# A decoder layer on one core: block sums moved from GpSimd to VectorE, the second half of x turned when it is due, gates stored before their sigmoid

## The chip, the core and the metric

The kernel runs on one core of a Trainium2 chip. A core has TensorE (PE: matrix products into PSUM, eight banks of 128 partitions x 512 float32), VectorE (DVE), ScalarE (ACT: functions and copies), GpSimd (POOL), and SyncE (SP), which here only issues transfers. Each engine works through its own queue in order; engines wait for each other by semaphores. The metric is the device time of one execution in microseconds (us), the median over the runs.

## The reference

One layer on a sequence of 1024 rows x 1024 columns, all in float32. x is normalised by row, scaled and shifted by vectors made from `c` (the modulation), and multiplied by a wide weight matrix `w_in`, whose columns are cut into ten parts. An attention branch (8 heads of 64, a mixture of three dilated windows) and a gated recurrence branch (8 heads of 128, in chunks) follow. Each is gated, multiplied by its own matrix, and the two are added under sigmoid gates `g_a` and `g_b`:

```python
h = rmsnorm(x, norm_g) * (1.0 + scale[:, None]) + shift[:, None]
proj = h @ w_in
q_a, k_a, v_a, z_a, q_b, f_b, i_b, z_b, g_a, g_b = jnp.split(proj, cuts, axis=-1)
o_a = dilated_attention(q_a, k_a, v_a, rel_bias) * silu(z_a)
o_b = rmsnorm(hgrn2_recurrence(silu(q_b), f_b, i_b, lb), hgrn_onorm_g) * silu(z_b)
y = sigmoid(g_a) * (o_a @ w_branch_a) + sigmoid(g_b) * (o_b @ w_branch_b)
return rmsnorm(x + gate[:, None] * (y @ w_out), final_g)
```

## The kernel before, in words

**Products in three parts.** A float32 product is made of three products of rounded parts: every operand is split into a high part (`hi`, an ACT copy to a rounded type) and a low part (`lo = a - hi`, a subtraction on DVE, helper `sub`, L224). `mm3` (L238 to L241) issues the three matrix instructions. Nearly all PE work is such 128x512 matrix instructions.

**Seven products for eight.** The projection h @ w_in is worked off in pairs of 128-column blocks (`add_pair`, L265): the 2x2 block product of weights and h takes seven products of 12 matrix instructions instead of eight. For that h, cut into blocks b11, b12 (first 512 columns of the model axis, first and second 512 rows), b21 and b22, is needed split, and with it four sums of blocks, t1 to t4, split as well. Weight sums (`w_s`) are made on DVE as each product is prepared.

**The stream.** The steps of all pairs stand in one queue, `stream`. `stream.step()` issues a quarter of a product (three matrix instructions) and prepares weights two products ahead. The attention and the recurrence, which have waits of their own, call `fill(amount)` between their parts, so that the PE gets a certain number of such steps there. `fill.rate` spreads the steps evenly; `fill.limit` (`in_attention`, `in_gating`) is how far the queue may go. The order of instructions on PE is as the code issues them. On the other engines a scheduler chooses the order, except between `region = ExitStack()` (L511) and `region.close()` (L773), where the written order holds there too.

**The stages**, with their times in the profile of before. (1) The start, 0 to 90 us: the eight row tiles of x are loaded, their row norms taken (`norm_x`), scaled (`scale_x`), transposed on PE (`turn_x`, two PSUM banks for a tile) and copied to `xt` (`keep_x`); the modulation comes from `w_ada` in four parts, each a `modulate(c)`: two halves of 16 small matrix records (`mod_row`), an ACT copy to a row, and a transposition by four tiny products (`mod_turn`). `make_h(j, th)` then makes one of 16 pieces of h and its split: ACT writes `hi`, DVE the value and `lo`. `first_products(j)` are 18 matrix instructions, for three blocks of 128 columns, as soon as piece j is there; all eight are 144. `bias_row` and `bias_add` make the table of the attention's bias. `warm(n)` issues idle products. (2) From 90 us the unit `"first"` (48 matrix instructions for the block VA+P), then the first pair, qk1. (3) Attention with filler, to about 474 us. (4) The branch product of a, with filler ahead of it, to about 560 us. (5) The recurrence with filler, to about 979 us. (6) The branch product of b, the merge and the output, to the end.

**What the change touches.** The sums t1 to t4 are made on GpSimd, in pieces of 128x512 (`sum_1`, `blocks`, `block_4`, L639 to L649), and split by `store_sum` (L634) on ACT and DVE. Two weight splits at the start have their `lo` on GpSimd too (`split_first(1, nc.gpsimd)`, L699, L701). The gates g_a and g_b go through a sigmoid as they leave PSUM (`ev_sigmoid`, L399) and are stored to DRAM (`ga_d`, `gb_d`); they are read back in `branch_a` (L960) and `branch_b` (L1182). The sigmoid and the attention's exponential (L859) need different tables on ACT, and a row ACT_TABLE_LOAD stands at each change between them.

Of the kernel before, what the change touches and what calls it, by code (L numbers as in the profile page):

```python
# [19 lines left out]
P = 128  # L20
# [159 lines left out]
def hybrid_layer(ctx: ExitStack, tc: tile.TileContext, x, w_ada, b_ada, w_in, w_branch_a, w_branch_b, w_out,  # L180
# [218 lines left out]
    def ev_sigmoid(dst, times=False):  # L399

        def ev(src, th, psum):
            t = ctile() if psum or times else src
            nc.scalar.activation(t, src, AF.Sigmoid)
            if times:
                out_ = t if psum else src
                nc.vector.tensor_tensor(out_, src, t, ALU.mult)
                t = out_
            nc.sync.dma_start(dst[:, half_of(th)], t)
        return ev
# [81 lines left out]
    add_unit(w_in_k, VA + P, lambda kh, th, k: [t[:, k] for t in X[NAMES[kh, th]]], ev_v(1), "first")  # L491
    stx = ExitStack()
    sp = stx.enter_context(tc.tile_pool(name="start", bufs=1, side="right"))
    with ExitStack() as st:
# [23 lines left out]
        xs = []  # L518
# [6 lines left out]
        def load_x(t):  # L525
            xs.append(lp.tile([P, D], F32, name=f"x{t}"))
            nc.sync.dma_start(xs[t], x[t * P:(t + 1) * P, :])
# [9 lines left out]

        def mod_row(c, a):
            ps = px.tile([P, 512], F32, name=("pmod", "pxt")[a])
            for k in range(KT):  # L540
                g = 32 * (k % 4)
                nc.tensor.matmul(ps[g:g + 32, 0:256], scz[:, k], was[c][2 * a + k // 4][:, k % 4],
                                 start=k < 4, stop=k >= 4)
            nc.scalar.copy(rows[a], ps[:, 0:256])

        def mod_turn(c, a):
            js = slice(2 * c, 2 * c + 2)
            ps = px.tile([P, 512], F32, name=("pmod", "pxt")[a])
            for n in range(2):
                nc.tensor.matmul(ps[:, n:n + 1], rows[a][:, n * P:(n + 1) * P], ones[:, 0:1], start=True, stop=True)  # L550
            if a == 0:
                nc.vector.tensor_tensor(mods[:, 0, js], ps[:, 0:2], b1[:, js], ALU.add)
                nc.vector.tensor_tensor(mods[:, 0, js], mods[:, 0, js], sm[:, C_G + 2 * c:C_G + 2 * c + 2], ALU.mult)
            else:
                nc.vector.tensor_tensor(mods[:, 1, js], ps[:, 0:2], sm[:, C_B + 2 * c:C_B + 2 * c + 2], ALU.add)

        def modulate(c):
            for a in range(2):
                mod_row(c, a)
            for a in range(2):  # L560
                mod_turn(c, a)

        def norm_x(t):
            if t % 2 == 0:
                nc.scalar.activation(junk[0], xs[t], AF.Square, accum_out=ss[:, t:t + 1])
            else:
                nc.vector.tensor_tensor_reduce(junk[1], xs[t], xs[t], 1.0, 0.0, ALU.mult, ALU.add, ss[:, t:t + 1])
            nc.vector.tensor_scalar(rs[:, t:t + 1], ss[:, t:t + 1], 1.0 / D, EPS, ALU.mult, ALU.add)
            nc.gpsimd.tensor_tensor(rs[:, t:t + 1], rs[:, t:t + 1], half[:, 0:1], ALU.pow)

        def scale_x(t):
            if t % 2:
# [4 lines left out]
        def split_first(n, engine=nc.vector):  # L577
            hi, lo = (wpool.tile([P, 4, P], F32R, name=name) for name in ("w_hi", "w_lo"))
            nc.scalar.copy(hi, stream.tiles[ids[n]])
            engine.tensor_tensor(lo, stream.tiles[ids[n]], hi.bitcast(F32), ALU.subtract)  # L580
# [34 lines left out]
        def make_h(j, th):  # L615
            hj = xt[th][:, j]
            hi, lo = X[NAMES[j // 4, th]]
            nc.scalar.activation(hi[:, j % 4], hj, AF.Identity, bias=mods[:, 1, j:j + 1], scale=mods[:, 0, j:j + 1])
            nc.vector.tensor_scalar(hj, hj, mods[:, 0, j:j + 1], mods[:, 1, j:j + 1], ALU.mult, ALU.add)
            sub(lo[:, j % 4], hj, hi[:, j % 4])  # L620
# [13 lines left out]
        def store_sum(name, k, got):  # L634
            hi, lo = X[name]
            nc.scalar.copy(hi[:, k], got)
            sub(lo[:, k], got, hi[:, k])

        def sum_1(k):  # L639
            t = ctile()  # L640
            nc.gpsimd.tensor_tensor(t, xt[1][:, k], xt[0][:, k], ALU.subtract)
            return t

        def blocks(k):
            nc.gpsimd.tensor_tensor(xt[1][:, k], xt[1][:, k + 4], xt[1][:, k], ALU.subtract)
            nc.gpsimd.tensor_tensor(xt[0][:, k], xt[1][:, k], xt[0][:, k], ALU.add)

        def block_4(k):
            nc.gpsimd.tensor_tensor(xt[0][:, k + 4], xt[0][:, k + 4], xt[0][:, k], ALU.subtract)  # L649
# [757 lines left out]
```

## Time and profile before

| | |
|---|---|
| median of 3 runs | 1168.54 us (1166.1 to 1171.85) |
| the profiled execution | 1164.41 us, span 1162.6 us |
| mean granted TensorE clock | 0.987 |
| PE busy | 1114.2 us, 96% of the span |
| DVE busy | 826.7 us, 71% |
| ACT busy | 549.7 us, 47% |
| POOL busy | 143.9 us, 12% |

The span runs from the first to the last instruction of one execution; its own time is 1.8 us longer, and 4.1 us under the median of the runs. How to read the lines that follow: a line of the waits reads "engine, its line of the code <- engine that released it: us in total, times, longest". A line of the timeline starts with the start and the duration in us; at its end, in brackets, stands how long the engine had been idle and what ended that. A matrix instruction's duration (0.39) overlaps with the next one's; the pitch from start to start is what it costs. A line of the windows gives, for a stretch of time, the busy time of each engine, the granted clock (PEclk, 1.00 is full) and the share of the transfer engines. A line of the groups gives the number of instructions, their busy time in all and the mean in ns. Line numbers (L239) are those of the code above.

### The profile page before, as it was taken

The page shows a single profiled execution, that of the slowest core. Times are in us where ns is not written, and L with a number is a line of the kernel's source. Part 1 is how long each engine was busy: PE and PEld are TensorE (multiplying, and loading weights), DVE is VectorE, ACT ScalarE, POOL GpSimd, SP SyncE. Part 2 cuts the span into 40 slices and gives each one's busy share as a digit, 9 for nine tenths or more (in the row PEclk, how much of TensorE's full clock was granted, in tenths as well). Part 3 has the DMA queues.
Part 4 walks back from the last instruction along what each step waited for, and adds up shares of the span by engine and source line. Part 5 has one row for each costly group of instructions (what it writes and reads, how often), then busy time and mean ns, then how long its engine had stood idle before and what let it go on. Part 6 is the DMA issues. An engine that isn't in the chain of part 4 may idle for free.

```text
span 1162.6 us, 21691 instructions
## 1 busy us (share of the span) xinstructions
PE 1114.2 (96%) x8278; PEld 912.2 (78%) x8278; DVE 826.7 (71%) x1622; ACT 549.7 (47%) x1080; POOL 143.9 (12%) x213
## 2 busy tenths in 40 slices
PE   4888999999999999989999999999999999999997
PEld 4666788887788877878877878788887878888886
DVE  4578877878767777753878787878878773679053
ACT  5335655587887876621343434343444433224021
POOL 2055212122122110200000000000000012000000
PEclk9888999999999999999999999999999999999999
DMA  9717776575455442775625354443525279874052
GB/s 319 210 38 215 189 205 169 149 171 143 114 154 159 109 132 76 234 237 185 205 87 182 101 165 147 135 163 103 185 83 180 98 228 324 290 227 144 15 179 75
DMA packets 161480, 189.54 MB, mean 163 GB/s; under 512 B 11312, under 2 KB 107696, under 8 KB 161376
## 3 DMA queue, kind: packets, MB, share of 16 engines
q1 hardware_dynamic: 140080, 153.95, 41.6%
q0 software_dynamic: 20896, 33.60, 11.4%
q8 instruction: 65, 1.06, 0.4%
q10 hardware_dynamic: 400, 0.61, 0.2%
q14 instruction: 39, 0.32, 0.1%
HBM read 129.36 MB, written 58.76 MB: 162 GB/s over the span
## 4 chain that ended last, share of the span: by engine, by line
PE 82%; DVE 4%; ACT 3%; issue 2%; DMA 1%; POOL 0%; POOLq 0%; ACTq 0%; DVEq 0%
PE m L239 17%; PE m L241 16%; PE m L240 16%; PE pq L240 5%; PE pq L239 5%; PE pq L241 5%; PE po L886 3%; PE pp L1042 2%; PE pt L871 2%; PE pss L854 1%; PE pss L853 1%; PE pou L1125 1%; PE pou L1127 1%; PE pou L1110 1%; DMA vq_d<-ct 1%
## 5 line engine op out<-in xcount | busy, mean ns | idle before, releaser
L246 ACT CAST w_hi<-w_raw 128x512 fp32r<-128x512 f32 x146 | 90.5, 622 | 99.3 <-PE m L241 52.6
L224 DVE TENSOR_TENSOR w_lo<-w_raw,w_hi 128x512 fp32r<-128x512 f32 x150 | 105.0, 702 | 40.4 <-ACT w_hi L246 39.7
L246 ACT CAST w_hi<-w_s 128x512 fp32r<-128x512 f32 x90 | 56.1, 623 | 84.4 <-PE m L241 66.7
L327 ACT COPY ct<-m 128x512 f32<-128x512 f32 x90 | 52.7, 585 | 83.3 <-PE m L241 70.6
L274 DVE TENSOR_TENSOR ct<-m,ct 128x512 f32<-128x512 f32 x90 | 61.9, 688 | 23.8 <-PE m L241 22.4
L224 DVE TENSOR_TENSOR w_lo<-w_s,w_hi 128x512 fp32r<-128x512 f32 x90 | 61.9, 687 | 5.7 <-ACT w_hi L246 5.3
L1133 POOL TENSOR_TENSOR ssh<-ssh,halfh 128x4 f32<-128x4 f32 x16 | 16.9, 1057 | 360.6 <-DVE ssh L1132 360.6
L224 DVE TENSOR_TENSOR ptl<-pt,pth 128x512 fp32r<-128x512 f32 (+1 forms) x80 | 50.6, 632 | 13.8 <-ACT pth L875 13.1
L859 ACT ACTIVATE s<-s,st 128x128 f32<-128x128 f32 (+3 forms) x64 | 49.7, 777 | 19.4 <-DVE st L856 19.1
L875 ACT CAST pth<-pt 128x512 fp32r<-128x512 f32 (+1 forms) x80 | 43.5, 543 | 28.3 <-PE pt L871 24.7
L239 PE MATMUL m<-t4h,w_hi 128*128 128x512 f32 x120 | 50.1, 417 | 3.0 <-DVE ct L274 3.0
L239 PE MATMUL m<-b11h,w_hi 128*128 128x512 f32 x124 | 51.7, 417 | 0.0
L239 PE MATMUL m<-t1h,w_hi 128*128 128x512 f32 x120 | 51.0, 425 | 0.0
L239 PE MATMUL m<-b21h,w_hi 128*128 128x512 f32 x124 | 50.9, 411 | 0.0
L239 PE MATMUL m<-b22h,w_hi 128*128 128x512 f32 x124 | 50.9, 410 | 0.0
L239 PE MATMUL m<-t3h,w_hi 128*128 128x512 f32 x120 | 50.2, 418 | 0.0
L856 DVE CUSTOM_DVE_ANT_0 s<-pss,toep 128x512 f32<-128x512 f32 (+2 forms) x64 | 37.3, 587 | 18.0 <-PE pss L854 17.9
L239 PE MATMUL m<-t2h,w_hi 128*128 128x512 f32 x120 | 49.6, 414 | 0.0
L836 POOL DMA_DIRECT2D k<-qk_d x64 | 34.9, 561 | 116.0 <-PE pss L854 112.8
L871 PE MATMUL pt<-kc,s 128*128 128x128 f32 x288 | 44.9, 272 | 4.1 <-DVE s L861 2.1
L241 PE MATMUL m<-b11l,w_hi 128*128 128x512 f32 x124 | 48.8, 393 | 0.0
L241 PE MATMUL m<-b22l,w_hi 128*128 128x512 f32 x124 | 48.7, 393 | 0.0
(352 smaller groups left out, 3299.9 us busy)
## 6 DMA issues: line engine op xcount, KB each, us to landing
w_raw<-in_w_in_dram SPq DMA_DIRECT2D x128, 256.0 KB, 3.3
wa<-in_w_ada_dram SPq DMA_DIRECT2D x16, 512.0 KB, 8.4
qk_d<-ct SPq DMA_DIRECT2D x32, 256.0 KB, 3.3
k<-qk_d POOLq DMA_DIRECT2D x64, 128.0 KB, 4.8
x<-in_x_dram SPq DMA_DIRECT2D x8, 512.0 KB, 7.3
qp<-qk_d POOLq DMA_DIRECT2D x32, 128.0 KB, 4.2
toep<-toep_d POOLq DMA_DIRECT2D x8, 512.0 KB, 6.4
vq_d<-ct SPq DMA_DIRECT2D x16, 256.0 KB, 5.2
```

What stands on the lines that cost most here:

```text
L224: nc.vector.tensor_tensor(out_, a, hi.bitcast(F32), ALU.subtract)
L239: nc.tensor.matmul(ps, ah, bh, start=start, stop=False, skip_group_check=more)
L240: nc.tensor.matmul(ps, al, bh, start=False, stop=False, skip_group_check=more)
L241: nc.tensor.matmul(ps, ah, bl, start=False, stop=stop, skip_group_check=more)
L246: nc.scalar.copy(hi, src)
L274: nc.vector.tensor_tensor(out_, a, b_, op)
L327: nc.scalar.copy(c[name], b[which])
L836: nc.gpsimd.dma_start(dst[c][E * hh:E * hh + E], qk_d[n + hh if dst is qp else n][r, half_of(c)].bitcast(F32R))
L856: nc.vector.tensor_tensor_reduce(s[:, ks:ks + w], ps[:, :w], toep[:, x0:x0 + w][:, ::-1], -1.0, prev, ALU.add, ALU.min, st2[:, a:a + 1])
L859: nc.scalar.activation(s[:, :kw], s[:, :kw], AF.Exp, bias=prev, scale=-1.0, accum_out=st2[:, 2:3])
L871: nc.tensor.transpose(pt[:, c0:c0 + P], pn[b][:, kt * P:(kt + 1) * P], ident)
L875: nc.scalar.copy(pth[:, :w], pt[:, :w])
```

## The change

Five things are changed.

1. t1 to t4 are made on DVE, in place in `xt`, in eight pieces of 128x1024 (`block_sum`). Each has three steps: difference on DVE, `hi` on ACT, `lo` on DVE. A call of `tick()` starts one more piece and does one step of each piece under way; the calls stand between the first products, the evictions and the first steps of the stream. The two weight splits move from GpSimd to DVE.
2. The second half of x (tiles 4 to 7) is loaded into the room of t4, scaled there, and turned late: `turn_late(j)` transposes the four 128x128 pieces that belong to piece j into one PSUM bank, and `make_h` reads that bank. `keep_x` is left out for this half. For j of 2 and over `make_h` makes the value and `hi` on ACT (two instructions) and only `lo` on DVE.
3. `modulate` keeps both halves in one PSUM bank, `pmod`, and turns them in it. The bias rows come before the first products; of the two `warm` calls one is left, at another place.
4. 29 steps of the stream are issued before the attention (16 before), inside the stretch where the order is as written; the pairs are declared earlier. Pair iz0 comes before fq0; the first pair of g_b moves from the recurrence into the attention's part, and fq0 from the attention's part to the one behind it. `fill(6)` becomes `fill(8)` ahead of the branch product of a.
5. g_a and g_b are stored without their sigmoid; it is taken on ACT when they are read. (`ev_silu` is what is left of `ev_sigmoid`.)

```diff
-    def ev_sigmoid(dst, times=False):
...
+    def ev_silu(dst):
         def ev(src, th, psum):
...
+    for m in (0, 2, 4, 6):
+        pair(GA + m * P, GA + m * P + P, ev_raw(ga_d[m]), ev_raw(ga_d[m + 1]))
+    pair(GB, GB + P, ev_raw(gb_d[0]), ev_raw(gb_d[1]))
+    pair_iz(0)
+    in_attention = len(stream.steps)
+    pair_fq(0)
+    pair_fq(1)
+    pair_iz(1)
+    in_gating = len(stream.steps)
...
         def mod_row(c, a):
-            ps = px.tile([P, 512], F32, name=("pmod", "pxt")[a])
+            if a == 0:
+                pmods[c] = px.tile([P, 512], F32, name="pmod")
+            ps = pmods[c][:, 256 * a:256 * a + 256]
...
+        def turn_late(j):
+
+            ps = px.tile([P, 512], F32, name="pxt")
+            for t in range(4):
+                nc.tensor.transpose(ps[:, t * P:t * P + P], xs[4 + t][:, j * P:(j + 1) * P], ident)
+            make_h(j, 1, ps)
...
+            s, b = mods[:, 0, j:j + 1], mods[:, 1, j:j + 1]
+            if j < 2:
+                nc.scalar.activation(hi[:, j % 4], got, AF.Identity, bias=b, scale=s)
+                nc.vector.tensor_scalar(hj, got, s, b, ALU.mult, ALU.add)
+            else:
+                nc.scalar.activation(hj, got, AF.Identity, bias=b, scale=s)
+                nc.scalar.copy(hi[:, j % 4], hj)
             sub(lo[:, j % 4], hj, hi[:, j % 4])
...
+            return [lambda: nc.vector.tensor_tensor(to, a, b_, ALU.subtract),
+                    lambda: nc.scalar.copy(hi[:, s], to), lambda: sub(lo[:, s], to, hi[:, s])]
+
+        sums = [(name, c) for name in ("t1", "t3", "t2", "t4") for c in range(2)]
+        under_way = []
+
+        def tick():
+
+            if sums:
+                under_way.append(block_sum(*sums.pop(0)))
+            for parts in under_way:
+                parts.pop(0)()
+            while under_way and not under_way[0]:
+                under_way.pop(0)
...
-    stream.need("first")
+    for steps in (10, 10, 9):
+        for _ in range(steps):
+            stream.step()
+        tick()
+    region.close()
...
-                fill(6)
+                fill(8)
...
                     nc.sync.dma_start(g[th], ga_d[m][:, half_of(th)])
+                    nc.scalar.activation(g[th], g[th], AF.Sigmoid)
...
                     nc.sync.dma_start(gb[th], gb_d[m][:, half_of(th)])
+                    nc.scalar.activation(gb[th], gb[th], AF.Sigmoid)
```

The order of the instructions, before and after, at three places. The first is PE at the second part of the modulation, `modulate(1)`; a bracket names the semaphores that an instruction waits for (DMAHW: a transfer; Activation: ACT). Before:

```order
L542 MATMUL pmod<-wa_166,scz 32x256 [waits DMAHW4_49]
L542 MATMUL pmod<-wa_166,scz 32x256 x3
L542 MATMUL pmod<-wa_168,scz 32x256 [waits DMAHW5_49]
L542 MATMUL pmod<-wa_168,scz 32x256 x3
L542 MATMUL pxt<-wa_170,scz 32x256 [waits DMAHW6_49,PE_49]
L542 MATMUL pxt<-wa_170,scz 32x256 x3
L542 MATMUL pxt<-wa_172,scz 32x256 [waits DMAHW7_49]
L542 MATMUL pxt<-wa_172,scz 32x256 x3
L550 MATMUL pmod<-ones,row_187 128x1 [waits Activation_49]
L550 MATMUL pmod<-ones,row_187 128x1
L550 MATMUL pxt<-ones,row_188 128x1 [waits Activation_49]
L550 MATMUL pxt<-ones,row_188 128x1
```

The same place of the changed kernel, where both halves stand in `pmod`:

```order
L572 MATMUL pmod<-wa_164,scz 32x256 [waits DMAHW4_49]
L572 MATMUL pmod<-wa_164,scz 32x256 x3
L572 MATMUL pmod<-wa_166,scz 32x256 [waits DMAHW5_49]
L572 MATMUL pmod<-wa_166,scz 32x256 x3
L572 MATMUL pmod<-wa_168,scz 32x256 [waits DMAHW6_49,Activation_49]
L572 MATMUL pmod<-wa_168,scz 32x256 x3
L572 MATMUL pmod<-wa_170,scz 32x256 [waits DMAHW7_49]
L572 MATMUL pmod<-wa_170,scz 32x256 x3
L582 MATMUL pmod<-ones,row_185 128x1 [waits Activation_49]
L582 MATMUL pmod<-ones,row_185 128x1
L582 MATMUL pmod<-ones,row_186 128x1 x2
```

The second half's products now wait for ACT (the copy of the first half's row), and the turning products wait for the copy of the second row.

The second place is DVE from the last piece of h to the weights of the first pair (t1l to t4l: low parts of the sums; `pm`: PSUM of the first products; L430: the eviction of q). Before:

```order
L224 TENSOR_TENSOR b22l<-xt_114,b22h 128x512
L224 TENSOR_TENSOR t1l<-ct,t1h 128x512 x4
L224 TENSOR_TENSOR w_lo<-w_raw_629,w_hi 128x512
L430 SCALAR_TENSOR_TENSOR ct<-pm_0_324,ct 128x512
L430 SCALAR_TENSOR_TENSOR ct<-pm_1_409,ct 128x512
L224 TENSOR_TENSOR w_lo<-w_raw_927,w_hi 128x512
L224 TENSOR_TENSOR ct<-pm_0_325,ct 128x512
L224 TENSOR_TENSOR w_lo<-w_s,w_hi 128x512
L224 TENSOR_TENSOR ct<-pm_1_410,ct 128x512
L274 TENSOR_TENSOR w_s<-w_s,w_raw_927 128x512
L224 TENSOR_TENSOR t2l<-xt_113,t2h 128x512 x4
L224 TENSOR_TENSOR t3l<-xt_114,t3h 128x512 x4
```

The same place of the changed kernel (L679: the difference of a sum; L427: the eviction of q):

```order
L224 TENSOR_TENSOR b22l<-xt_114,b22h 128x512
L224 TENSOR_TENSOR t1l<-xt_113,t1h 128x1024
L679 TENSOR_TENSOR xt_114<-xt_114 128x1024
L224 TENSOR_TENSOR t1l<-xt_113,t1h 128x1024
L679 TENSOR_TENSOR xt_114<-xt_114 128x1024
L224 TENSOR_TENSOR w_lo<-w_raw_545,w_hi 128x512
L224 TENSOR_TENSOR t3l<-xt_114,t3h 128x1024
L679 TENSOR_TENSOR xt_113<-xt_114,xt_113 128x1024
L427 SCALAR_TENSOR_TENSOR ct<-pm_0_313,ct 128x512
L427 SCALAR_TENSOR_TENSOR ct<-pm_1_409,ct 128x512
L224 TENSOR_TENSOR t3l<-xt_114,t3h 128x1024
L679 TENSOR_TENSOR xt_113<-xt_114,xt_113 128x1024
```

The differences now stand among the low parts on DVE, and t3 has moved ahead of the evictions of q.

The third place is PE around the attention's first score (L853 and L854 before, L894 and L895 after; `t1h`, `t3h`: sums of blocks in the products of the pair qk1). Before:

```order
L239 MATMUL m_1002<-t1h,w_hi 128x512
L240 MATMUL m_1002<-t1h,w_lo 128x512
L241 MATMUL m_1002<-t1l,w_hi 128x512
L853 MATMUL pss<-k_911,qp_909 128x128
L854 MATMUL pss<-k_913,qp_909 128x128
L239 MATMUL m_1002<-t1h,w_hi 128x512
```

After:

```order
L241 MATMUL m_1011<-b21l,w_hi 128x512
L894 MATMUL pss<-k_978,qp_976 128x128
L895 MATMUL pss<-k_980,qp_976 128x128
L239 MATMUL m_856<-t3h,w_hi 128x512
L240 MATMUL m_856<-t3h,w_lo 128x512
L241 MATMUL m_856<-t3l,w_hi 128x512
```

The first score, which stood inside the pair's second product, now stands behind its fifth.

More of the change, by code (lines that the diff above doesn't have):

```diff
@@ L536, in load_wa, with mod_turn @@
                     was[c].append(w)
+        pmods = {}
         def mod_row(c, a):
-            ps = px.tile([P, 512], F32, name=("pmod", "pxt")[a])
+            if a == 0:
+                pmods[c] = px.tile([P, 512], F32, name="pmod")
+            ps = pmods[c][:, 256 * a:256 * a + 256]
             for k in range(KT):
                 g = 32 * (k % 4)
-                nc.tensor.matmul(ps[g:g + 32, 0:256], scz[:, k], was[c][2 * a + k // 4][:, k % 4],
+                nc.tensor.matmul(ps[g:g + 32], scz[:, k], was[c][2 * a + k // 4][:, k % 4],
                                  start=k < 4, stop=k >= 4)
-            nc.scalar.copy(rows[a], ps[:, 0:256])
-        def mod_turn(c, a):
+            nc.scalar.copy(rows[a], ps)
+        def mod_turn(c):
             js = slice(2 * c, 2 * c + 2)
[L548 to L555, printed above, removed]
+            ps = pmods[c].rearrange("p (a b) -> p a b", a=2)
+            for a in range(2):
+                for n in range(2):
+                    nc.tensor.matmul(ps[:, a, n:n + 1], rows[a][:, n * P:(n + 1) * P], ones[:, 0:1], start=True, stop=True)
+            nc.vector.tensor_tensor(mods[:, 0, js], ps[:, 0, 0:2], b1[:, js], ALU.add)
+            nc.vector.tensor_tensor(mods[:, 1, js], ps[:, 1, 0:2], sm[:, C_B + 2 * c:C_B + 2 * c + 2], ALU.add)
+            nc.vector.tensor_tensor(mods[:, 0, js], mods[:, 0, js], sm[:, C_G + 2 * c:C_G + 2 * c + 2], ALU.mult)
         def modulate(c):
@@ L559, in modulate, with square_x @@
                 mod_row(c, a)
[L560 to L564, printed above, removed]
+            mod_turn(c)
+        def square_x(t, on_act):
+            if on_act:
                 nc.scalar.activation(junk[0], xs[t], AF.Square, accum_out=ss[:, t:t + 1])
@@ L686, in main_banks @@
                 main[u, th] = pm.tile([P, 512], F32, name=f"pm{u}_{th}")
-        for f, t in all_of_x(0):
-            pass
+        norm_x(0)
+        scale_x(0)
+        turn_x(0)
+        norm_x(1)
+        keep_x(0)
+        scale_x(1)
+        turn_x(1)
+        norm_x(2)
+        keep_x(1)
+        norm_x(3)
+        scale_x(2)
+        turn_x(2)
+        split_first(0)
+        for b in range(2):
+            bias_row(b)
+        scale_x(3)
+        turn_x(3)
+        keep_x(2)
+        for b in range(2):
+            bias_add(b)
@@ new lines, in hybrid_layer @@
+        bias_row(2)
+        keep_x(3)
+        bias_add(2)
+        split_first(1)
+        modulate(0)
+        load_wa(2)
+        split_first(2)
+        make_h(0, 0)
+        make_h(1, 0)
+        main_banks(0)
+        for u in range(3):
+            first_products(0, (0,), (u,))
+        first_products(1, (0,))
+        square_x(4, True)
+        root_x(4)
+        square_x(5, True)
+        square_x(7, False)
+        root_x(5)
+        root_x(7)
+        scale_x(4)
+        square_x(6, True)
@@ L690, in hybrid_layer @@
+        scale_x(5)
+        root_x(6)
+        scale_x(7)
+        scale_x(6)
         warm(8)
[L691 to L693 removed]
+        turn_late(0)
         for a in range(2):
[L695 to L708 removed]
@@ L919, in hybrid_layer @@
         fill.limit = in_gating
-        fill.rate = in_attention * 4 / NH / sum((j + 1) * w for j, w in enumerate(ATT_W))
+        fill.rate = (in_attention - stream.at) * 4 / NH / sum((j + 1) * w for j, w in enumerate(ATT_W))
         fill(2.0)
@@ L1003, in load_f @@
         def load_f(h):
+            stream.need(f"f{h}")
             stream.need(f"h{h}")
```

207 lines of the change are left out of this document (82 added, 125 removed).

## The prediction

> **What bounds the kernel now.** I read the page's first table, then what PE waited for, then the windows, then the timeline where the waits lie.
>
> ```profile
> span 1162.6 us, 21691 instructions
> PE 1114.2 (96%) x8278; PEld 912.2 (78%) x8278; DVE 826.7 (71%) x1622; ACT 549.7 (47%) x1080; POOL 143.9 (12%) x213
> ```
>
> PE is the bound: it is busy for all but 1162.6 - 1114.2 = 48.4 us. The change leaves its matrix products as they are, so it can win only idle time of PE and time in which PE ran at less than its full clock. PE's waits say where the idle time lies, the windows where the clock was low:
>
> ```profile
> PE pm L594 <- DVE x L575: 14.2, 4, 7.5
> PE pt L450 <- DVE ct L224: 4.4, 2, 4.2
> PE po L886 <- DVE oa L892: 3.2, 6, 0.8
> PE m L239 <- DVE ct L274: 3.0, 1, 3.0
> ...
> PE pt L871 <- DVE s L861: 2.1, 2, 1.1
> PE pt L871 <- ACT ct L470: 2.0, 1, 2.0
> ...
> PE pt L1139 <- DVE kt L1134: 1.3, 1, 1.3
> ```
>
> ```profile
> core 0: us, PE busy (x) PEld busy (x) DVE busy (x) ACT busy (x) POOL busy (x), PEclk, DMA share, GB/s
> 30.00:40.00 10.00, 8.04 (x36) 6.67 (x37) 5.56 (x11) 3.60 (x6) 2.39 (x4) 0.72 1.12 327
> 70.00:80.00 10.00, 7.36 (x25) 5.46 (x24) 8.76 (x10) 5.14 (x9) 6.28 (x4) 0.67 0.11 31
> 100.00:110.00 10.00, 5.81 (x31) 4.70 (x29) 9.62 (x18) 7.90 (x18) 4.18 (x8) 0.87 1.20 272
> 110.00:120.00 10.00, 8.71 (x36) 6.81 (x35) 5.40 (x17) 4.31 (x13) 2.85 (x4) 0.79 1.02 273
> 500.00:510.00 10.00, 7.31 (x27) 5.89 (x28) 5.21 (x9) 2.70 (x5) 0.00 (x0) 0.83 0.78 246
> 700.00:800.00 100.00, 100.00 (x1181) 81.81 (x1180) 81.58 (x158) 42.69 (x98) 4.03 (x4) 1.00 0.44 143
> ```
>
> The loss stands in the first 120 us and once near 500 us; from 700 to 800 us PE was never idle. I take the change stage by stage.
>
> **1. The start, from the first product to the unit "first".** These lines of the timeline give the two ends, the waits between them and the prices:
>
> ```profile
> 18.89 1.95 PE L613 MATMUL pmod<-ones 128*128 128x128 f32 x16
> 25.17 0.48 PE L628 MATMUL pm<-b11h,w_hi 128*128 128x512 f32 x1
> ...
> 31.14 1.97 PE L594 MATMUL pm<-kc,x 128*128 128x128 f32 x8 [3.12 <-DVE x L575]
> ...
> 39.48 1.06 PE L594 MATMUL pm<-kc,x 128*128 128x128 f32 x8 [0.82 <-DVE x L575]
> ...
> 45.45 1.07 PE L542 MATMUL pmod<-wa,scz 128*32 128x256 f32 x16
> ...
> 46.33 1.05 PE L542 MATMUL pxt<-wa,scz 128*32 128x256 f32 x16
> ...
> 47.31 0.61 PE L550 MATMUL pmod<-ones,row 128*128 128x1 f32 x4
> ...
> 48.34 0.48 PE L628 MATMUL pm<-b12h,w_hi 128*128 128x512 f32 x1
> ...
> 50.61 0.81 PE L655 MATMUL pmod<-oh,rb 32*8 32x384 f32 x2
> 51.99 0.50 PE L628 MATMUL pm<-b11h,w_hi 128*128 128x512 f32 x1
> ...
> 69.54 0.61 PE L631 MATMUL pm<-b21l,w_hi 128*128 128x512 f32 x1 [1.15 <-DVE b21l L224]
> ...
> 75.09 0.63 PE L631 MATMUL pm<-b21l,w_hi 128*128 128x512 f32 x1
> 75.52 0.63 PE L628 MATMUL pm<-b22h,w_hi 128*128 128x512 f32 x1
> ...
> 90.34 0.39 PE L239 MATMUL m<-b11h,w_hi 128*128 128x512 f32 x1
> ...
> 101.33 1.03 PE L450 MATMUL pt<-kc,ct 128*128 128x128 f32 x8
> ```
>
> Prices: at full clock a 128x512 instruction costs (101.33 - 90.34) / 48 = 0.229, at the half clock 75.52 - 75.09 = 0.43; four transpositions cost 1.06 / 2 = 0.53; a bias row (51.99 - 50.61) / 2 = 0.69; a `modulate` 48.34 - 45.45 = 2.89.
>
> In the changed order each `modulate` is a chain. The first half takes 46.33 - 45.45 = 0.88; then the second half waits until the first row is copied, which by the rows lasts 47.31 - 46.33 = 0.98; the second half takes 0.88 and waits 0.98 again; the turning takes 48.34 - 47.31 = 1.03. That is 4.75, or 1.86 more each. Nothing covers it: the products behind it stand in PE's own queue.
>
> First product: 25.17 + 3 x 0.69 for the bias rows that now come ahead + 1.86 for `modulate(0)` - 1.95 for the `warm(8)` that is gone from there = 27.15. (The `warm(6)` only filled a wait.) From there PE has 144 instructions x 0.229 = 33.0; eight `turn_late` x 0.53 = 4.2; three `modulate` x 4.75 = 14.2; a warm(8) at full clock, half of 1.95, 1.0; and waits. One wait I see: tile 6 is scaled last, behind four squares, its root on POOL and two scalings; between 0 (hidden under the 4 us of the first 18 products) and the 3.12 that tile 4 cost before I take 1.8, since the first three tiles are ahead of it. Sum: 27.15 + 54.2 = 81.3.
>
> What else could hold PE here? ACT makes two instructions of a piece instead of one; the prices are here, with those of DVE for the sums:
>
> ```profile
> L403 ACT ACTIVATE ct<-ct 128x512 f32<-128x512 f32 x46 | 29.1, 633 | 12.5 <-DVE ct L274 11.6
> L403 ACT ACT_TABLE_LOAD x20 | 25.7, 1283 | 0.4
> L859 ACT ACT_TABLE_LOAD x20 | 25.7, 1283 | 0.4
> ```
>
> ```profile
> 101.22 2.49 DVE L224 TENSOR_TENSOR t3l<-xt,t3h 128x512 fp32r<-128x512 f32 x4
> ```
>
> ```profile
> 71.45 1.59 POOL L646 TENSOR_TENSOR xt<-xt,xt 128x512 f32<-128x512 f32 x1
> 71.84 1.75 DVE L224 TENSOR_TENSOR b22l<-xt,b22h 128x512 fp32r<-128x512 f32 x1
> ```
>
> Four ACT instructions of about 0.63 for the two halves of a piece are 2.5 us, under the 18 x 0.229 = 4.1 of its products: hidden, each `turn_late` finding its bank read. On DVE a low part costs 2.49 / 4 = 0.62 alone and 1.75 beside GpSimd's sum. The sums and their low parts are 16 instructions of 2 x 0.62 = 1.25, 20.0 us; with about 26 others of 0.62 (low parts of h and of weights, evictions) DVE has 36 us of work between the last four pieces and the pair's third product, in some 44 us. It fits, without the low parts that took 1.75.
>
> Last, the clock. Before, it was low twice in this stretch: (1 - 0.72) x 10 = 2.8 and (1 - 0.67) x 10 = 3.3 us lost. The second time it fell behind a wait of only 1.15 us, among the small products of a `modulate`. The new chains of 4.75 us hold more idle time than that, so I expect one such fall, 3.05, to the bounds of none and of all 144 instructions at 0.43 (29). The unit then starts at 84.3 instead of 90.34: **-6.0** (from -9.1 to +20).
>
> The Trainium skill ("TensorE: Matmul & The Clock Gate", Part 1) has PE fall to half its clock only after an idle window of some 3.4 us; the trace differs, with 1.15 us at 69.54. By that rule no wait above would cost clock, and the sum would be 3.05 lower.
>
> **2. From the unit to the end of the pair's third product.** Before, from 90.34 to the start of the fourth:
>
> ```profile
> 109.30 1.09 PE L450 MATMUL pt<-kc,ct 128*128 128x128 f32 x4 [4.19 <-DVE ct L224]
> ...
> 120.70 0.39 PE L239 MATMUL m<-b22h,w_hi 128*128 128x512 f32 x1
> ...
> 502.69 0.47 PE L239 MATMUL m<-t4h,w_hi 128*128 128x512 f32 x1 [2.98 <-DVE ct L274]
> ```
>
> This is 30.4 us. In it lie the wait of 4.19 for DVE, whose queue held t2 to t4, 1.1 for the first softmax, and by the clocks 0.87 and 0.79 (windows 100 and 110) 1.3 + 2.1; without them 21.7. In the changed order the sums stand ahead of these rows and GpSimd does not slow them; PE works through five whole products before the first score, so the score's loads have about 10 us more. DVE still has some ten instructions of 0.62 ahead of the first score, and PE reaches the softmax's transposition about as soon: I leave the 1.1 as it is and add 1 for low parts that come late. -8.7 + 2.1 = **-6.6**. If DVE or the loads of the head are no earlier than today, PE waits as before: 0.
>
> **3. The attention.** ACT loads tables 20 + 20 times here; in the changed order I count 13 loads in the whole program. About 28 x 1.28 = 36 us of ACT's time go, and 24 sigmoids of 0.63 with them. ACT is no bound, so only the waits count in which PE stood behind it: po behind oa 3.2 (an ACT copy stands ahead of oa) and pt behind s 2.1. I take **-2.0** of these 5.3; the 2.0 behind L470 stays, since iz0 is still last here; on the other side stand 20 filler steps less, at worst one more wait of 2.0.
>
> **4. The branch of a.** At 502.69 PE had run out of filler: of two pairs behind `in_attention` 52 steps can be issued, the attention takes about 18 of them in advance, and 8 x `fill(6)` asks for 48 more. Now three pairs give 80, some 12 are taken, and 8 x `fill(8)` asks for 64 of 68. The wait of 2.98 and the clock of 0.83 behind it, 1.7, go: **-4.7**. Bounds: 0, if DVE waits for the transfers of z and oa as before; the sigmoids of g_a (16 x 0.63) wait for a load each in ACT's queue, with weights' high parts behind them, and could cost up to the 2.98 again.
>
> **5. The rest: 0.** A pair fewer in the recurrence: PE's work for it moves, it is not saved; PE is busy there throughout, at worst one more wait like L1139's 1.3. g_b's sigmoids: 16 x 0.63 of ACT, which is at 43% from 700 to 800 us and lower behind 1000; each is prepared two steps ahead.
>
> **Sum**: -6.0 - 6.6 - 4.7 - 2.0 = -19.3. The profiled execution, 1164.4, would become 1145.1; the median of the runs lies 4.1 above it, so I predict 1168.5 - 19.3 = **1149.2**.
>
> **The rivals.**
>
> (a) The early gain is given back at the first scores: PE arrives earlier, and waits for DVE or for the loads of head 0, and the branch of a keeps its wait. For: DVE was at 9.62 of 10 there, and its order behind the written stretch is the scheduler's. Against: 36 us of work in 44. Left are -6.0 - 2.0: 1160.5.
>
> (b) The clock does not fall at all in stage 1: 1146.2, and with the whole 5.3 of the attention's waits 1143.
>
> (c) Slower: the clock stays at half from the first product to the end of the unit, 192 instructions, because the chains of `modulate` and the single bank of `turn_late` keep breaking PE's work. Each costs 0.20 more, in all 38.4 instead of 3.05: 1168.5 - 19.3 + 35.3 = 1184.5. It decides from (19.3 + 3.05) / 0.20 = 112 of the 192. For: the fall at 69.54 behind 1.15 us. Against: the row at 75.52 lasts 0.63 and that at 90.34 only 0.39, so the clock came back between them, within 15 us, with the chains of the last pieces still going on. The Trainium skill ("TensorE: Matmul & The Clock Gate", "A second HAM failure mode") tells of such a case, PE idling briefly between groups in PSUM banks so that its clock swings; no run here shows it.
>
> (d) No change that can be told: (a), with two more falls of the clock: -8.0 + 6.1 = -1.9, 1166.6.
>
> **How the numbers follow.** A forecast as summed, 0.50; (a) 0.18; (b) 0.17; (c) 0.05; (d) 0.10. A difference under 0.5% (5.8 us) can hardly be told from none with runs that spread over 5.7. Forecast, (a) and (b) are faster, but (a) by only 8.0, so I give a little of it to no change: faster 0.84, same 0.10, slower 0.06. The range reaches from (b) with all of the attention's waits, 1143, less 1.5 for stage 2 without its new wait, to (a) with a wait of 1.3 more: 1141 to 1162.
>
> **What would show it.** Each right: the unit's first L239 near 84 us; no GpSimd sums and no low part of 1.75; b22's first product of qk1 about 12 us earlier than 120.70; 13 table loads; no wait of 3 us on t4 at 500 us. Wrong: a granted clock under 0.8 in most windows from 30 to 90 us, a new wait of several us at the first pss or pt, or PE waiting for a weight's high part in the branch of a.

## The result and the profile after

| | before | changed |
|---|---|---|
| median of 6 runs | 1168.78 us | 1150.82 us (1147.99 to 1151.76) |
| ratio to before, 95% interval | | 0.9841 (0.9823 to 0.986) |
| profiled execution, span | 1164.41, 1162.6 | 1151.74, 1149.9 |
| PE busy | 1114.2 us, 96% | 1113.1 us, 97% |
| table loads on ACT | 43 | 13 |

The change is faster by 1.6%, some 18 us; 1149.2 was forecast. The two profiled executions differ by 12.7 us only: that of before is 4.4 under its median, that of the changed kernel 0.9 above. The terms can be compared only inside these two, so their sum is held against 12.7, and the other 5.3 us are not located.

Some of PE's waits in the changed kernel (each `modulate` waits twice for a row copy, at L582 and, with the same figures, at L572):

```profile
PE pmod L582 <- ACT row L574: 2.0, 4, 0.5
...
PE pt L1182 <- DVE kt L1177: 2.0, 2, 1.3
PE pt L465 <- DVE zs L1184: 1.4, 2, 0.9
```

The waits on oa (3.2) and on v's split (4.4) are nearly or wholly gone; the row copies (L574) are new. The windows by stage, of before and then of the changed kernel (unit "first" to 140 us, attention, branch of a, the rest):

```profile
90.34:140.00 49.66, 44.18 (x207) 36.19 (x206) 42.42 (x87) 29.13 (x62) 15.32 (x21) 0.93 0.83 221
140.00:475.00 335.00, 327.50 (x1742) 273.54 (x1741) 256.12 (x587) 240.85 (x428) 60.33 (x104) 0.99 0.52 142
475.00:545.00 70.00, 67.02 (x288) 54.26 (x287) 40.18 (x63) 21.00 (x36) 7.92 (x15) 0.98 0.76 245
560.00:1162.60 602.60, 593.04 (x5580) 485.51 (x5578) 425.94 (x784) 216.21 (x484) 30.03 (x41) 1.00 0.48 157
```

```profile
85.90:140.00 54.10, 50.10 (x228) 40.19 (x227) 44.55 (x85) 29.88 (x60) 10.20 (x18) 0.97 0.77 225
140.00:475.00 335.00, 334.47 (x1793) 282.11 (x1791) 262.61 (x602) 199.76 (x394) 67.38 (x118) 1.00 0.57 153
475.00:545.00 70.00, 67.55 (x288) 54.40 (x289) 36.74 (x57) 28.81 (x52) 0.11 (x1) 0.98 0.63 203
560.00:1149.90 589.90, 577.87 (x5508) 471.90 (x5506) 415.92 (x772) 211.67 (x479) 31.19 (x41) 1.00 0.49 158
```

Length less the first busy time is PE's idle time: 5.5 and 4.0, 7.5 and 0.5, 3.0 and 2.5, 9.6 and 12.0 (from 545 to 560 us PE is never idle in either kernel). The clock column adds about 1.7 of loss for a half-clock window in before's attention and in each of the two branch stages. So the attention, of which 2.0 was expected, gave 7.0 + 1.7 = 8.7, and the branch of a, of which 4.7 was expected, gave 0.5.

The timeline of PE at the start, changed:

```profile
16.04 1.97 PE L627 MATMUL pm<-kc,x 128*128 128x128 f32 x8 [2.79 <-DVE x L610]
17.94 1.44 PE L698 MATMUL pxt<-oh,rb 32*8 32x384 f32 x2
...
23.86 1.94 PE L572 MATMUL pmod<-wa,scz 128*32 128x256 f32 x16
26.29 1.94 PE L572 MATMUL pmod<-wa,scz 128*32 128x256 f32 x16 [0.49 <-ACT row L574]
28.72 1.87 PE L582 MATMUL pmod<-ones,row 128*128 128x1 f32 x8 [0.49 <-ACT row L574]
32.01 0.79 PE L666 MATMUL pm<-b11h,w_hi 128*128 128x512 f32 x1 [1.42 <-ACT b11h L653]
...
36.04 0.39 PE L669 MATMUL pm<-b11l,w_hi 128*128 128x512 f32 x1
...
40.94 1.07 PE L572 MATMUL pmod<-wa,scz 128*32 128x256 f32 x16
...
44.98 0.42 PE L638 MATMUL pxt<-kc,t4h 128*128 128x128 f32 x2
...
45.37 0.47 PE L666 MATMUL pm<-b12h,w_hi 128*128 128x512 f32 x1
...
85.90 0.39 PE L239 MATMUL m<-b11h,w_hi 128*128 128x512 f32 x1
```

The first half of a modulation lasts 1.94 at 23.86 and 1.07 at 40.94, and a product takes 0.39 only from 36.04 on: until then PE ran at half its clock. A modulation costs 44.98 - 40.94 = 4.04 at full clock, the first one 28.72 + 1.87 - 23.86 = 6.7; a `turn_late` 45.37 - 44.98 = 0.39. From 36 us on no stretch ran at half clock until the first scores:

```profile
108.16 0.50 PE L239 MATMUL m<-b22h,w_hi 128*128 128x512 f32 x1
...
119.80 0.30 PE L912 MATMUL pt<-kc,s 128*128 128x128 f32 x1 [1.13 <-DVE s L902]
121.23 0.60 PE L912 MATMUL pt<-kc,s 128*128 128x128 f32 x2 [1.13 <-DVE s L902]
...
122.26 0.63 PE L239 MATMUL m<-b11h,w_hi 128*128 128x512 f32 x1
```

b22's product starts 12.5 us earlier than the 120.70 of before (12.6 forecast), but the softmax's waits, one of which stood ahead of that mark before, now stand behind it, with a half-clock window.

Ahead of the branch of a, the timeline of PE, and of ACT at the same time:

```profile
485.22 0.47 PE L239 MATMUL m<-b11h,w_hi 128*128 128x512 f32 x1 [2.01 <-DVE ct L274]
```

```profile
482.61 0.63 ACT L1008 ACTIVATE oar<-oar 128x512 f32<-128x512 f32 x1 [4.26 <-DMA oar<-ga_d]
483.15 0.60 ACT L997 CAST oah<-oar 128x512 fp32r<-128x512 f32 x1
```

ACT stood 4.26 us for the load of g_a whose sigmoid (L1008) comes ahead of a high part of oa (L997); DVE waited for that, and the eviction that PE needed (L274) was queued behind it on DVE.

### The profile page after: what moved, and what is told of

Read it like the earlier page. It is cut to its first block, busy times and chain, and to the rows that moved or that the text cites. A ratio compares the mean times of both kernels' runs of the same rounds, so it can differ in the third digit from the quotient of the medians.

```text
span 1149.9 us, 21616 instructions
## 1 busy us (share of the span) xinstructions
PE 1113.1 (97%) x8266; PEld 908.7 (79%) x8266; DVE 809.0 (70%) x1607; ACT 517.8 (45%) x1059; POOL 117.7 (10%) x195
## 4 chain that ended last, share of the span: by engine, by line
PE 82%; DVE 7%; issue 6%; DMA 2%; ACT 2%; POOL 1%; ACTq 0%; POOLq 0%; DVEq 0%; SPq 0%
PE m L239 16%; PE m L241 15%; PE m L240 15%; PE pq L240 5%; PE pq L239 5%; PE pq L241 5%; PE pp L1085 3%; PE po L927 2%; PE pt L912 2%; PE pss L895 1%; PE pss L894 1%; PE pou L1168 1%; PE pou L1170 1%; PE pou L1153 1%; PE pmod L572 1%
## 5 line engine op out<-in xcount | busy, mean ns | idle before, releaser
L274 DVE TENSOR_TENSOR ct<-m,ct 128x512 f32<-128x512 f32 x90 | 61.8, 687 | 27.7 <-PE m L241 26.1
L916 ACT CAST pth<-pt 128x512 fp32r<-128x512 f32 (+1 forms) x80 | 43.6, 544 | 36.3 <-PE pt L912 31.9
L240 PE MATMUL m<-b11h,w_lo 128*128 128x512 f32 x124 | 49.2, 397 | 0.0
L240 PE MATMUL m<-b21h,w_lo 128*128 128x512 f32 x124 | 48.6, 392 | 0.2 <-DVE w_lo L224 0.2
L241 PE MATMUL m<-b21l,w_hi 128*128 128x512 f32 x124 | 48.8, 393 | 0.0
```

Of the source, the lines that this page charges most:

```text
L240: nc.tensor.matmul(ps, al, bh, start=False, stop=False, skip_group_check=more)
L241: nc.tensor.matmul(ps, ah, bl, start=False, stop=stop, skip_group_check=more)
L274: nc.vector.tensor_tensor(out_, a, b_, op)
L916: nc.scalar.copy(pth[:, :w], pt[:, :w])
```

## The experiments

Ratios are to the kernel before; the changed kernel has 0.9841. With intervals of about ±0.0016, a difference between two kernels under 0.0024 (2.8 us) isn't shown by the times alone; there the profile decides, and the text says so. Two of the texts on record give 7.5 and 7.0 us as the idle time before between 140 and 450 us; it is 5.5 there, and 7.5 up to 475 us, which is the window read below.

| | what | median us | ratio | interval |
|---|---|---|---|---|
| e1 | sigmoid at the eviction again | 1155.67 | 0.9903 | 0.9889 to 0.9917 |
| e2 | old order of the pairs | 1150.70 | 0.9854 | 0.9837 to 0.9872 |
| e3 | sums on GpSimd | 1149.39 | 0.9846 | 0.9833 to 0.9859 |
| e4 | modulation in two banks | 1146.02 | 0.9819 | 0.9804 to 0.9834 |
| e5 | sigmoids of g_a late | 1146.55 | 0.9821 | 0.9804 to 0.9838 |
| e6 | idle products ahead | 1147.60 | 0.9825 | 0.9807 to 0.9843 |
| e7 | sums in a lump | 1157.74 | 0.9917 | 0.9902 to 0.9932 |
| e8 | scores earlier | 1149.85 | 0.9842 | 0.9824 to 0.9861 |
| e9 | before, raw gates alone | 1164.99 | 0.9968 | 0.9954 to 0.9982 |
| e10 | 16 steps | 1151.57 | 0.9849 | 0.9833 to 0.9865 |
| e11 | e4 + e5 + e6 | 1142.03 | 0.9772 | 0.9757 to 0.9788 |
| e12 | e11, scaling ahead | 1147.04 | 0.9815 | 0.9798 to 0.9831 |

**e1: point 5 undone.**

```diff
-        pair(GA + m * P, GA + m * P + P, ev_raw(ga_d[m]), ev_raw(ga_d[m + 1]))
+        pair(GA + m * P, GA + m * P + P, ev_sigmoid(ga_d[m]), ev_sigmoid(ga_d[m + 1]))
...
-                    nc.scalar.activation(g[th], g[th], AF.Sigmoid)
```

> The changed kernel with the sigmoids of g_a and g_b taken again as they leave PSUM (point 5 undone, all else as changed). The attention's stretch (140 to 450 us) held 0.5 us of PE idle time in the changed kernel and 7.5 us before. Theory A, the table loads of ScalarE were behind those waits: some 20 to 30 more table loads than the 13, PE idle in that stretch 4 us or more, the wait of 2.0 us at 485 us (a sigmoid of g_a waiting for its load) and the half clock behind it gone; in all 2 to 5 us slower than the changed kernel, 1153 to 1156. Theory B, the new order of the pairs and the longer queue took the waits away: idle there under 2 us, and the wait at 485 us gone, so 3 to 4 us faster than the changed kernel, about 1147.

It is 0.0062 slower than the changed kernel, 7.2 us, more than A's 2 to 5, with 45 table loads for 13. The window of the attention, ACT's timeline in it, and PE's:

```profile
140.00:475.00 335.00, 328.78 (x1757) 276.54 (x1757) 256.32 (x589) 244.31 (x432) 63.26 (x110) 0.99 0.56 147
```

```profile
353.70 1.28 ACT L397 ACT_TABLE_LOAD   x1
354.99 0.64 ACT L397 ACTIVATE ct<-ct 128x512 f32<-128x512 f32 x1
355.64 1.28 ACT L907 ACT_TABLE_LOAD   x1
356.94 1.15 ACT L907 ACTIVATE s<-s,st 128x1024 f32<-128x1024 f32 x1
...
358.20 0.37 ACT L939 COPY t<-po 64x256 f32<-64x256 f32 x1
```

```profile
359.54 0.39 PE L934 MATMUL po<-pth,vq 128*128 128x256 f32 x1 [3.67 <-DVE oa L940]
```

The idle time is 6.2 again instead of 0.5. Here the whole chain of one wait can be read: a sigmoid of 0.64 between two exponentials costs two loads of 1.28, and the copy (L939) that DVE's L940 needs to free PE's bank stands behind all of it, while PE is idle for 3.67. ACT was busy 244 of 335 us and did not bound anything on average. The Trainium skill ("ScalarE: Activation LUTs", "What ACT_TABLE_LOAD costs") gives 1283 ns for the load and some 2.66 us for a whole switch, with a drain; the rows differ, since the sigmoid starts 1.29 after its load began, and the next load begins 0.01 after the sigmoid ends.

**e9: point 5 alone, in the kernel before** (the reverse of e1's edit, in the old order).

> The kernel before with point 5 alone (gates stored without sigmoid, sigmoid taken when they are read). Theory A, table loads of ScalarE were behind the attention's waits: PE idle from 140 to 450 us falls from 7.0 to under 2 us and the half clock at 458.7 goes, while a sigmoid that waits for its load now stands in ScalarE's queue near 500 us, where PE's wait of 3.0 becomes 3 to 6; in all 4 to 9 us faster than before, 1158 to 1163. Theory B, the order of the steps did it: idle there over 5 us, 1165 to 1169.

```profile
140.00:475.00 335.00, 329.19 (x1759) 276.53 (x1758) 257.49 (x592) 208.33 (x398) 61.31 (x105) 0.99 0.52 142
```

It gives 0.0032 (3.7 us), less than A said, and PE's idle time falls only from 7.5 to 5.8. So raw gates are worth 5.7 us of idle time in the changed kernel and 1.7 in the old one, where a wait of 2.0 for the pair iz0 (457 us), two for scores and one of 1.1 on oa remain. They need the rest of the change to pay in full; neither theory holds alone.

The wait at 457 us is the same chain, but the sigmoid in it is that of iz0's own columns z, which raw gates leave in place. ACT and PE in e9, then that sigmoid in the changed kernel:

```profile
451.31 0.64 ACT L403 ACTIVATE ct<-ct 128x512 f32<-128x512 f32 x1
...
452.82 1.28 ACT L859 ACT_TABLE_LOAD   x1
```

```profile
457.00 0.55 PE L871 MATMUL pt<-kc,s 128*128 128x128 f32 x3 [2.03 <-ACT ct L470]
```

```profile
441.08 0.63 ACT L402 ACTIVATE ct<-ct 128x512 f32<-128x512 f32 x1
```

In e9 the last exponential comes behind it (454.12) and needs a load, as in the kernel before (454.91); in the changed kernel the last one started at 435.41, ahead of it. In e1 and e2 too it comes ahead, so neither the gates nor the order of the pairs did it. These three kernels share points 1 to 3, the 29 steps, and a line of the change that reckons `fill.rate` from the steps still to come (`in_attention - stream.at`); no run takes these apart.

**e2: the order of the pairs undone.**

```diff
-    pair(GB, GB + P, ev_raw(gb_d[0]), ev_raw(gb_d[1]))
+    pair_fq(0)
     pair_iz(0)
     in_attention = len(stream.steps)
-    pair_fq(0)
     pair_fq(1)
...
-                fill(8)
+                fill(6)
```

> The changed kernel with the old places of the pairs and fill(6) (of point 4 only the 29 steps stay). Theory A (table loads made the attention's waits): idle in the attention stays under 1.5 us; ahead of the branch product of a the filler runs out, with a wait of 2 to 3 us near 500 us and half a clock window, 1.7; in all 0 to 4 us slower than the changed kernel, 1151 to 1155. Theory B (the order did it): 4 us or more of idle time return in the attention besides, 1156 to 1160.

```profile
475.00:545.00 70.00, 65.72 (x280) 52.70 (x279) 34.52 (x52) 24.86 (x44) 1.06 (x2) 0.98 0.66 214
```

0.0013 slower, inside the intervals. The idle time in the attention is 1.25, so theory B falls; ahead of the branch of a it is 70.00 - 65.72 = 4.3 against 2.5 of the changed kernel, a wait of 2.6 on t4 near 489 us and one of 1.7 for a weight's low part. ACT's sigmoids of g_a wait for loads there too, and the run doesn't part the two causes. By these windows the order of the pairs is worth 0.7 + 1.8 us of idle time.

**e5: the sigmoids of g_a behind their products**, with ACT's order as written there.

```diff
-                    nc.scalar.activation(g[th], g[th], AF.Sigmoid)
...
             def ev(ps, th, psum):
+                nc.scalar.activation(g[th], g[th], AF.Sigmoid)
...
-        stream.need("ya")
+        with tc.manual_schedule(engines={mybir.EngineType.Activation}):
+            stream.need("ya")
```

> The changed kernel with the sigmoids of g_a put behind their products, in the written order of ScalarE, so that none stands ahead of the last high parts of oa. If the wait of 2.0 us at 485 us and the half clock behind it (1.7) came from a sigmoid waiting for its load, both go: PE idle from 450 to 545 us falls from 2.5 to under 1 us, in all 2 to 4 us faster than the changed kernel, 1146 to 1148 beside its 1149 to 1151. Rival, the high parts of oa wait for the transfers of z and oa themselves, and the wait stays: within 1 us.

```profile
475.00:545.00 70.00, 69.56 (x306) 56.50 (x305) 38.46 (x60) 27.99 (x51) 0.00 (x0) 1.00 0.66 211
```

The idle time falls from 2.5 to 0.4 and the clock column to 1.00: the 2.0 + 1.7 at 485 us came from that sigmoid. The time, 0.0020 lower, is what this adds up to, if not beyond the intervals by itself.

ACT's wait for g_a stands in other variants too, a little shorter, and PE's wait at that place shrinks faster than it: 4.26 and 2.01 in the changed kernel, 3.99 and 1.40 in e4, 3.82 and 0.48 in e3, 3.39 and none in e6. So the 2.0 + 1.7 come and go with less than 1 us of ACT's wait, and the times of e3, e6 and e10 hold a gain at this place which their edits did not aim at.

**e3: the differences on GpSimd again**, `nc.vector` to `nc.gpsimd` in `block_sum`'s first step.

> The changed kernel with the eight differences of the block sums issued on GpSimd again, in the same three spaced steps. Theory S, GpSimd's slow sums were behind the early wait: a sum of 128x1024 takes about 2 x 1.59 = 3.2 us there, the low parts beside it 2 x 1.75 = 3.5 us instead of about 1.3, DVE comes late, PE waits 4 us or more between 75 and 125 us, total 1154 to 1158. Rival, the spacing and the early start of the sums did it and the engine is of no matter: PE's idle time up to 125 us within 1.5 us of the changed kernel's, total 1149 to 1152.

Four of that line's eight instructions (the other four read much the same), changed kernel and then e3 (least, median and greatest ns, first and last start), and e3's window from 86 us:

```profile
L679 DVE TENSOR_TENSOR xt<-xt x4: 1216/1218/1219, 81.1 to 95.5; 128x1024 f32<-128x1024 f32 x4
```

```profile
L679 POOL TENSOR_TENSOR xt<-xt x4: 2387/2899/3392, 71.1 to 92.4; 128x1024 f32<-128x1024 f32 x4
86.00:140.00 54.00, 49.32 (x228) 38.77 (x227) 45.53 (x82) 28.97 (x58) 20.00 (x22) 1.00 0.77 225
```

A difference takes 2.9 instead of 1.2, and a low part beside it up to 3.4 instead of 1.2, as the theory had it; yet the time is the same and PE's idle time 4.7 instead of 4.0. The clock did not fall at the first scores here (1.00 against 0.97). That the sums left GpSimd is worth 0.7 us of idle time in this window, and nothing that the time can tell.

**e7: t3, t2 and t4 in one lump behind the evictions**, on DVE.

```diff
+        for name in ("t3", "t2", "t4"):
+            for c in range(2):
+                for part in block_sum(name, c):
+                    part()
```

> The changed kernel with t3, t2 and t4 made in one lump on VectorE, behind the last evictions, as they stood in the queue before; t1 stays as changed. If the place and the spacing of the sums, not the engine, made the early gain, VectorE then has six pieces of about 2.6 us, 15 us, ahead of the first weights' low parts of qk1, and PE waits 4 to 8 us between 86 and 115 us: total 1154 to 1159. Rival, the steps are of no matter since VectorE has room: within 2 us, 1149 to 1152.

ACT's timeline and PE's:

```profile
103.46 1.04 ACT L680 CAST t4h<-xt 128x1024 fp32r<-128x1024 f32 x1 [2.43 <-DVE xt L679]
106.93 1.04 ACT L680 CAST t4h<-xt 128x1024 fp32r<-128x1024 f32 x1 [2.43 <-DVE xt L679]
107.88 0.61 ACT L246 CAST w_hi<-w_raw 128x512 fp32r<-128x512 f32 x1
```

```profile
108.55 0.80 PE L239 MATMUL m<-b11h,w_hi 128*128 128x512 f32 x1 [10.32 <-ACT w_hi L246]
```

0.0076 slower, 8.9 us. Without the spacing each piece is a chain DVE, ACT, DVE of 106.93 - 103.46 = 3.47, six of them in a row, and the next weights' high part stands behind the last on ACT, not on DVE as the text on record had it. So the place and the spacing of the sums, which this run changes together, carry this part of the change; the engine (e3) doesn't.

**e10: 16 steps in the written stretch** instead of 29, `(6, 5, 5)` for `(10, 10, 9)`.

> The changed kernel with 16 steps of the stream in the written stretch instead of 29 (6 + 5 + 5), as many as before. If the longer written stretch is what keeps the weights of qk1 and the sums in the right order on VectorE and ScalarE, PE waits 3 us or more between 86 and 125 us besides the 3.7 of now, and the time is 1153 to 1157. Rival, the spacing of the sums alone does it: within 2 us of the changed kernel, 1149 to 1152.

```profile
86.00:140.00 54.00, 48.57 (x224) 39.64 (x223) 47.02 (x93) 30.19 (x62) 11.87 (x22) 0.94 0.76 207
```

The time is 0.0008 higher, not told apart. In this window PE loses 5.4 - 4.0 = 1.4 us more and one clock window of 1.7 more (0.94 against 0.97), about the 3 us of the theory; in the branch of a it is idle for 0.4 instead of 2.5 and the clock doesn't fall: ACT waits 2.78 for g_a there, and PE not at all. The longer stretch helps where it stands, and the end doesn't show it.

**e8: less filler ahead of the first score, more behind.**

```diff
-        fill(2.0)
+        fill(0.5)
         for _ in begin(0):
-            fill(0.5)
+            fill(1.25)
```

> The changed kernel with less filler ahead of the first score and more behind each of the first two (0.5 + 1.25 + 1.25 for 2.0 + 0.5 + 0.5). If PE's two waits of 1.13 us for the first softmax, and the clock window behind them (1.7), are only a matter of too little filler, they go: 2 to 4 us faster, 1146 to 1149. Rival, the first score waits for its loads instead: a wait of 1 to 3 us at the first pss, no gain.

The same time. The trace was taken at a granted clock of 0.66 and doesn't show whether the waits moved; that stays open.

**e4: two banks for the modulation.**

```diff
-            ps = pmods[c][:, 256 * a:256 * a + 256]
+            ps = px.tile([P, 512], F32, name=("pmod", "pxt")[a])[:, 0:256]
```

> The changed kernel with the two halves of each part of the modulation in two PSUM banks again. If the single bank makes the chain: a modulation at full clock falls from 4.04 to 2.9 us, the first (at half clock) from 6.7 to about 5.5, the waits of about 0.5 on the row copies go, the unit first starts 3 to 5 us earlier than 85.90, total 1146 to 1148. Rival, the second bank is the one that turn_late writes, so that the modulation now waits for the eviction of a piece of h, or a clock window falls: unit start within 1.5 us of 85.90, total 1149 to 1152.

```profile
25.68 1.64 PE L569 MATMUL pxt<-wa,scz 128*32 128x256 f32 x16
...
83.39 0.39 PE L239 MATMUL m<-b11h,w_hi 128*128 128x512 f32 x1
```

The waits of 0.49 on the row copies are gone, and the clock rises in the middle of the second half (1.64 between 1.94 and 1.05). The unit starts 2.5 us earlier, under the 3 to 5 expected: the clock then fell for the first products, which last 0.63 from 31.6 to 36.3 us, and the second modulation waits 0.72 for a piece of h in the second bank (`pxt`, at 41.97 us), as the rival had it. The time, 0.0022 lower, does not show the gain by itself.

**e6: eight idle products ahead of the bias rows**, `warm(8)` behind the third tile.

> The changed kernel with eight idle products of 128x128 (2 us at half clock) put behind the third tile's transpositions, at about 18 us, where the kernel before had its warm(8) a little later. If the clock stays at half until 35.6 us because the bias rows and the modulation are too small to raise it, it now rises near 18 to 22 us, the bias rows and the first modulation (6.7 us) take about 4 to 5 us less, and with the 2 us of the products themselves the first product starts 2 to 4 us earlier than 32.01; total 1146 to 1149. Rival, the small products let the clock fall again at once, or the start waits for loads: first product within 1 us of 32, total 1150 to 1152.

```profile
17.59 2.83 PE L645 MATMUL pxt<-ones 128*128 128x128 f32 x16
20.47 0.81 PE L698 MATMUL pxt<-oh,rb 32*8 32x384 f32 x2
...
23.62 1.07 PE L572 MATMUL pmod<-wa,scz 128*32 128x256 f32 x16
...
83.06 0.39 PE L239 MATMUL m<-b11h,w_hi 128*128 128x512 f32 x1
```

The bias rows take 0.81 instead of 1.44 and half a modulation 1.07 instead of 1.94; after the 2.83 us that the idle products take themselves, the unit still starts 2.8 us earlier, although the first products again run at half clock, from 31.1 to 32.8 us. So products of 128x128 raised the clock where the small ones had not. That smallness alone kept it low isn't shown: in e4 it rose during the modulation with no product added. The time, 0.0016 lower, can't be told by itself, and it holds the missing wait at 485 us (see e5).

**e11: e4, e5 and e6 together.**

> The changed kernel with e4, e5 and e6 together: two banks for the modulation, eight idle products ahead of it, the sigmoids of g_a behind their products. The start's two add up in part, since both shorten the first modulation: the unit first near 80 to 81 us (83.39 and 83.06 each alone, 85.90 changed); with the wait at 485 us gone, 1140 to 1144, and a ratio to before of 0.977 to 0.980. Rival, the start's two give the same 2.8 us and no more: 1144 to 1146.

```profile
80.18 0.39 PE L239 MATMUL m<-b11h,w_hi 128*128 128x512 f32 x1
```

0.9772: faster than before by 2.3% and than the changed kernel by 0.7%, with intervals that do not touch. It is the best version here. The start's two add up: the unit is 85.90 - 80.18 = 5.7 us earlier, for 2.5 and 2.8 of each alone.

**e12: the scaling of tiles 4 to 7 ahead of the first modulation**, and the later `warm(8)` out.

> As e11, and the squares, roots and scalings of tiles 4 to 7 ahead of the first modulation, where ScalarE and VectorE are idle from 18 to 28 us, and the warm(8) behind the first 18 products taken out. If the late scaling is what that warm(8) covers, PE goes from the 18 products straight to turn_late: 2 to 3 us faster than e11, 1138 to 1142. Rival, the scaling delays the first piece of h, or the clock falls without the idle products: same as e11 or slower.

ACT's timeline, then PE's:

```profile
24.80 1.06 ACT L591 ACTIVATE junk<-t4h 128x1024 bf16<-128x1024 f32 x1
```

```profile
31.20 0.61 PE L579 MATMUL pmod<-ones,row 128*128 128x1 f32 x4 [4.40 <-ACT row L571]
```

5 us slower than e11. ACT is idle there, but its order is as written, so the squares and scalings stand ahead of the two row copies, and PE waits 4.4 us for these; the first copy starts at 30.80. Behind that wait the first products run at half clock until 38.8 us (to 32.3 in e11).

## Why the prediction was right, and where not

The median was met within 1.6 us, in good part by luck: in the two profiled executions the terms add up to -13.2 where -19.3 was forecast for them, and the rest of the medians' 18.0 is not located. The direction was forecast rightly, and so were most of the mechanisms; the sizes were not. By the profiled executions:

- **Start**, -6.0 forecast, -4.4 measured (84.3 against 85.90). Two errors nearly cancel. The first product came at 32.01, not 27.15, since the step "Sum: 25.17 + ... - 1.95" priced the bias rows and the first modulation at full clock; without the `warm(8)` ahead of them they ran at half. The fall that was put in at 3.05 and the wait of 1.8 for tile 6 did not come. A modulation's chain cost 4.04, not 4.75 (PE waits 0.49 for a row copy), a `turn_late` 0.39, not 0.53, and a `warm(8)` 2.0, not 1.0: the 1.95 of the row at 18.89 was already a full-clock price. From the first product to the unit PE is idle for 3.3 us instead of 11.0: of the waits for tiles and low parts that the prediction lists there none is left. That the late turning did this is read from the two timelines; no run undoes it alone.
- **Unit to the third product**, -6.6 forecast, -8.1 to that mark. Part of it is given back behind the mark, where the first scores now stand: up to 140 us the idle time falls by 1.5 and the half-clock loss by about 0.6, in all 2.1. The step that failed is the choice of the mark: it left the first scores' waits out. This is rival (a) in part. And the 1.3 + 2.1 for the clock counted time in which PE waited anyway; the instructions that ran at half clock lost about 2.3.
- **Attention**, -2.0 forecast, -8.7 measured. The mechanism, PE behind ACT's changes of table, is borne out; its size is not. The step that failed is "the 2.0 behind L470 stays": that wait went, and with it a clock window of 1.7 that was not counted, 3.7 of the 8.7 (see e9; which part of the change moved iz0's sigmoid is open). Of the other 5.0 the raw gates alone bring 1.7 (e9), the rest only together with the rest of the change (5.7 in e1).
- **Branch of a**, -4.7 forecast, -0.5 measured. The wait on t4 shrank from 2.98 to 0.44, as forecast, and the bound that the prediction named, a sigmoid of g_a waiting for its load in ACT's queue, came in its place with 2.0 + 1.7 (e5).
- **The rest**, 0 forecast, +2.5 measured: waits of the recurrence (L1182, L465) in the list above; no run took them apart.

The sum of these, with 2.1 for the second, is -13.2, near the 12.7 of the spans. Rival (c) was right in part, up to 36 us and not beyond: with the two gaps of the modulation's chain closed the clock rises sooner (e4), but some eight products at half clock are far from the 112 from which it decides.

## What to carry to other kernels

An engine that is far from the busiest can still be the one waited for: look at what stands ahead of the instruction that frees a buffer, and take what needs another table on ACT out of the stretch that uses the first one. When an operation moves to the place where its operand is read, place it behind the load's arrival, since everything behind it in that engine's queue waits too. Long sums may be slow, if they start early and each step of a piece stands apart from the next.

## What the runs showed of the hardware

PE was busy without a gap from 16.04 to 25.80 and yet at half clock until 35.6: the transpositions, bias rows with 8 columns and modulation products with 32 did not raise it by then. With eight idle products of 128x128 among them it was full by 20.47, 4.6 us after PE began (e6); without the two gaps of 0.49 it rose in the modulation's second half, some 10 us after (e4). What decides between these isn't shown. The Trainium skill ("TensorE: Matmul & The Clock Gate", Part 1) has the clock full after some 3.4 us of sustained work; the changed kernel's trace differs, with 9.8 us. The windows' clock column reads 1.00 in this stretch: only the durations of like instructions show a clock that has been low from the start.
